# One visit for all eight chunks: regrouping the small products of a chunked recurrence beside a stream of projections

## The chip, the cores and the metric

One NeuronCore of one Trainium2 chip. The metric is the device time of one launch in microseconds. A core has five engines with queues of their own: TensorE (PE; its weight loads are shown as PEld), VectorE (DVE), ScalarE (ACT), GpSimd (POOL) and SyncE (SP). Each works through its queue in order; they meet at semaphores.

## The reference

A two-layer encoder over 512 tokens of width 1024. In each layer five branches read the same input h, each is gated and projected, and their sum goes through an output projection and a layer norm. Four branches are attention of some kind. The branch that matters here is a recurrence with a state S of 64 x 64 per head, for eight heads, run forward in time (e = 0) and backward (e = 1):

```
sa_t = S a_t
S    = S * w_t + sa_t b_t^T + v_t k_t^T
y_t  = S r_t
```

Here a = -kk (the normalised key), w is the decay, b = kk times a gate, and k is the key scaled by that gate. The two directions' outputs are added, normalised per head, and gated. The merge is

```
terms.append(sigmoid(h @ w_gate_i + b_gate_i) * (branch_i @ w_branch_i))
```

## The kernel before

All matmuls of the projections split each float32 operand into two parts and add three products of 512 columns (`gemm3_steps`, lines 149 to 151); the weights are loaded by SP (line 125) and split by ACT (line 135) and DVE (line 136). The tile framework allocates buffers by tag and orders each engine's queue ahead of time by a schedule of its own that follows the program's order where several instructions are ready.

**The recurrence** (`recurrence()`, from line 716) takes the 512 tokens in eight chunks of 64, two heads (128 partitions) at a time. A unit is one pair of heads `p` in one direction `e`; there are eight units in a layer. Within a chunk the recurrence becomes small matrix products and the inverse of a triangular 64 x 64 matrix; between chunks a state is carried.

- `pair_start(p)` projects k, r and v of the pair (`mixed`, lines 734 to 740).
- `early(p, e)` (line 802) makes the decays: running sums (line 820), the sums before and after each step (lines 824 to 833, tiles `bef`, `aft`), their exponentials, and the operands A0 and BK. Then, for two halves `c2` of four chunks each, the score products (line 881) go into two PSUM banks, `ps_s()` (tag psc, two banks) and `ps_m()` (tag pm, one bank). ACT copies 32-row blocks of them into NS (lines 890, 893), DVE masks the rest into MB and OM (lines 894, 896), and MB times the values goes into another `ps_m()` (line 902, helper line 92) and from there into Z (line 903). After both halves it makes B2 and K2, the operands at a chunk's end: `comp` through Exp (line 908), and products with it (lines 910, 912). They are transposed (line 921) and copied into OM (line 927).
- `late(p, e)` (line 945) inverts the 32-wide diagonal blocks of all chunks at once in a loop of 31 steps on DVE (lines 956 to 965, first transpose line 953), extends them to 64 (lines 978 to 990), and then, again for two halves of four chunks: px = WD x Z (line 1009) copied into WA and UV (lines 1012, 1015), WA x OM (line 1024) plus A0 into PE_ (line 1027), OM x UV (line 1035), and then the chain of states, chunk after chunk: a product of PE_ with the last state ST (line 1042), and its copy into the other ST by ACT and DVE (lines 1044, 1045). The results go to SY. px, both products of line 1024 and that of line 1035 use `ps_t()` (tag pt, two banks).
- `finish(p)` (line 1058) adds the outputs and gates them. It uses the bank pm too.

**The order of the work** is written by hand with generators. Every `yield` in these functions is a place where one step of other work is put in: the driver calls `pull(1)` (line 1114), which takes one step, three matmuls, from `fill()` (line 396), the gate and output projections of the other four branches (`branch_steps`, line 370; its PSUM bank is tag pf, its gating lines 380 to 390). A layer has 368 such steps: 8 output blocks times (8 + 4) for three branches and (8 + 2) for one. The attention part pulls 27 of them earlier by fractions (lines 623 and 702). What is left when the recurrence has ended runs at once (lines 1115, 1116), and then follow the projections of the recurrence's own branch and the output projection. In the recurrence `late(units[n])`, `finish` of the pair before, and `early(units[n + 1])` take turns, a yield each:

```
1106  while live:
1107      for g in list(live):
1108          if next(g, 0) == 0:
1109              live.remove(g)
1110          else:
1111              yield
```

Yields of a layer: 3 for each pair_start, 14 for each early, 24 for each late, 5 for each finish (4 for the last): 12 + 112 + 192 + 19 = 335.

Tiles of 128 x 512 in early() come from one rotating set, `tmp` (line 713), of 6 buffers.

## Time and profile before

| | |
|---|---|
| median of 3 runs | 2260.67 us (2260.49 to 2261.9) |
| the profiled execution | 2261.37 us |
| its span, first to last instruction | 2259.6 us |
| granted TensorE clock | 0.999 of full speed |
| recurrence of layer 0, and of layer 1 | 524 to 1032 us, 1623 to 2131 us |
| one pair of units, as an example | 714 to 842 us |

Busy time is the share of a stretch in which an engine executed an instruction; for PE the ends of matmuls are modelled, so the starts of successive ones tell more. In a row of a group, "x16 | 11.0, 685 | 0.0" is the count, the busy time in us, the mean of one in ns, and the idle time before them.

### The profile page before, as it was taken

To read this page: it belongs to the slowest core of one execution; us is meant where nothing else is said; L and a number is where in the kernel's file an instruction comes from. 1 tells how busy PE (TensorE), PEld (TensorE's weight loads), DVE (VectorE), ACT (ScalarE), POOL (GpSimd) and SP (SyncE) were. 2 spreads that over 40 slices of the span, in tenths; PEclk is the share of its full clock that TensorE was granted. 3 is DMA by queue.
4 is the path that set the end of the run, shared out by engine and by line. 5 is a ranking of instruction groups with operands and counts; after the bars stand their busy time and mean duration, and the time that the engine had idled before them with its cause. 6 is when DMAs were issued, how large, how long until landed. Compare 5 with 4: busy or idle time off the path is not lost.

```text
span 2259.6 us, 36239 instructions
## 1 busy us (share of the span) xinstructions
PE 2186.5 (97%) x13056; PEld 1678.6 (74%) x13056; DVE 1730.6 (77%) x4236; ACT 1273.2 (56%) x2785; POOL 59.6 (3%) x117
## 2 busy tenths in 40 slices
PE   6999999999999999999999999999999999999998
PEld 5777777777767777777787777777777777777776
DVE  7677887677989797975568778766788979879565
ACT  3565666676665555644326656677675646565440
POOL 0000000100000000000000000001000000000000
PEclk9999999999999999999999999999999999999999
DMA  7732124322222221315333312333313213222261
GB/s 261 222 108 91 56 80 112 113 86 85 75 80 66 86 88 59 102 49 181 117 115 108 98 62 70 97 106 89 112 57 99 71 62 98 72 80 73 84 195 38
DMA packets 111780, 220.49 MB, mean 98 GB/s; under 512 B 13240, under 2 KB 23224, under 8 KB 111216
## 3 DMA queue, kind: packets, MB, share of 16 engines
q1 hardware_dynamic: 101456, 195.09, 27.0%
q0 software_dynamic: 10144, 23.08, 4.0%
q8 instruction: 103, 1.69, 0.3%
q14 instruction: 77, 0.63, 0.1%
HBM read 187.66 MB, written 27.31 MB: 95 GB/s over the span
## 4 chain that ended last, share of the span: by engine, by line
PE 70%; DVE 14%; ACT 8%; DMA 5%; issue 3%; DVEq 0%; POOL 0%; ACTq 0%; SPq 0%
PE pg L150 10%; PE pg L151 10%; PE pg L149 10%; PE pf L149 6%; PE pf L150 5%; PE pf L151 5%; PE psc L444 4%; PE po L489 3%; PE pt L470 3%; DVE W L965 2%; DVE pr L963 2%; DMA wrawr<-in_w_out_dram 1%; DVE wlof L136 1%; PE po L479 1%; DMA wrawf<-in_w_mem_dram 1%
## 5 line engine op out<-in xcount | busy, mean ns | idle before, releaser
L149 PE MATMUL pg<-hT,whir 128*128 128x512 f32 (+1 forms) x912 | 364.0, 399 | 3.2 <-DVE kl L436 1.4
L150 PE MATMUL pg<-hT,whir 128*128 128x512 f32 (+1 forms) x912 | 365.4, 401 | 0.5 <-DVE hT L176 0.5
L151 PE MATMUL pg<-hT,wlor 128*128 128x512 f32 (+1 forms) x912 | 363.8, 399 | 2.1 <-DVE wlor L136 2.1
L136 DVE TENSOR_TENSOR wlor<-wrawr,whir 128x512 fp32r<-128x512 f32 x240 | 163.9, 688 | 114.8 <-ACT whir L135 104.9
L135 ACT CAST whir<-wrawr 128x512 fp32r<-128x512 f32 x240 | 147.7, 618 | 175.1 <-PE pg L150 116.7
L135 ACT CAST whif<-wrawf 128x512 fp32r<-128x512 f32 (+1 forms) x272 | 164.4, 605 | 135.4 <-PE pf L150 77.9
L149 PE MATMUL pf<-hT,whif 128*128 128x512 f32 x512 | 220.8, 431 | 3.4 <-DVE gt L388 2.8
L136 DVE TENSOR_TENSOR wlof<-wrawf,whif 128x512 fp32r<-128x512 f32 (+1 forms) x272 | 181.4, 669 | 49.2 <-ACT whif L135 43.2
L150 PE MATMUL pf<-hT,whif 128*128 128x512 f32 x512 | 206.7, 404 | 0.0
L151 PE MATMUL pf<-hT,wlof 128*128 128x512 f32 x512 | 205.2, 401 | 0.0
L149 PEld LDWEIGHTS pg<-hT,whir 128*128 128x128 f32 x912 | 172.0, 189 | 40.6 <-issue 3.0
L151 PEld LDWEIGHTS pg<-hT,wlor 128*128 128x128 f32 x912 | 171.9, 188 | 40.0 <-DVE wlor L136 4.9
L150 PEld LDWEIGHTS pg<-hT,whir 128*128 128x128 f32 x912 | 171.9, 189 | 37.8 <-issue 3.9
L176 DVE TENSOR_TENSOR pT<-pt,pT 128x512 fp32r<-128x512 f32 x176 | 114.2, 686 | 34.2 <-ACT pT L175 33.1
L175 ACT CAST pT<-pt 128x512 fp32r<-128x512 f32 x176 | 94.7, 589 | 63.0 <-PE pt L470 61.7
L149 PEld LDWEIGHTS pf<-hT,whif 128*128 128x128 f32 x512 | 96.5, 188 | 35.8 <-DVE gt L388 10.2
L470 PE MATMUL pt<-cst,p 128*128 128x128 f32 x704 | 118.6, 273 | 0.5 <-DVE p L461 0.5
L151 PEld LDWEIGHTS pf<-hT,wlof 128*128 128x128 f32 x512 | 96.4, 188 | 22.2 <-issue 1.6
L963 DVE TENSOR_TENSOR pr<-W,U 128x60 f32<-128x60 f32 (+24 forms) x496 | 103.5, 209 | 11.4
L965 DVE TENSOR_TENSOR W<-W,pr 128x60 f32<-128x60 f32 (+24 forms) x496 | 102.9, 208 | 11.0
L470 PEld LDWEIGHTS pt<-cst,p 128*128 128x128 f32 x704 | 89.8, 141 | 28.4 <-DVE p L461 3.6
L150 PEld LDWEIGHTS pf<-hT,whif 128*128 128x128 f32 x512 | 96.8, 189 | 18.8 <-issue 4.3
(326 smaller groups left out, 4809.1 us busy)
## 6 DMA issues: line engine op xcount, KB each, us to landing
wrawr<-in_w_in_dram SPq DMA_DIRECT2D x224, 256.0 KB, 2.8
wrawf<-in_w_gate_dram SPq DMA_DIRECT2D x160, 256.0 KB, 2.8
o<-scr_o POOLq DMA_DIRECT2D x26, 512.0 KB, 4.5
wrawf<-in_w_branch_dram SPq DMA_DIRECT2D x48, 256.0 KB, 2.7
bias<-scr_toe SPq DMA_DIRECT2D x24, 448.0 KB, 3.3
scr_o<-os SPq DMA_DIRECT2D x20, 512.0 KB, 3.7
wrawf<-in_w_in_dram SPq DMA_DIRECT2D x32, 256.0 KB, 3.0
wrawr<-in_w_out_dram SPq DMA_DIRECT2D x32, 256.0 KB, 2.9
```

The lines of the kernel that those rows point to most:

```text
L135: nc.scalar.copy(hi, raw)
L136: tt(lo, raw, f(hi), ALU.subtract)
L149: mm(ps, ah, bh, start=(i == 0), stop=False)
L150: mm(ps, ah, bl, start=False, stop=False)
L151: mm(ps, al, bh, start=False, stop=(i == n - 1))
L175: nc.scalar.copy(hi, src)
L176: tt(lo, src, f(hi), ALU.subtract)
L444: mm(ps[:, :nk], q[:, i, sl], part[:, i if g is None else g, :nk], start=(j == 0), stop=(j == 1))
L470: nc.tensor.transpose(pt[:, qb * 128:(qb + 1) * 128], p4[qb][:, kb * 128:(kb + 1) * 128], ident)
L489: mm(po, vwin(kb), pT[:, b, :], start=(kb == 0 and b == 0), stop=(kb == nkb - 1 and b == 1))
L963: tt(pr, W[:, t8, s:s + 1].to_broadcast([128, nt, n]), U[:, s:s + 1, rsl].to_broadcast([128, nt, n]), ALU.mult)
L965: tt(W[:, t8, rsl], W[:, t8, rsl], pr, ALU.add)
```

## The change

Four things. (1) In early() the score products of all eight chunks are made in one go, into four PSUM banks (psc, pm, psc, pg) where it was two banks for four chunks, and MB times the values goes into one bank and leaves it in one copy. MB is taken from the tmp set, whose buffers go from 6 to 5. (2) Of `bef` and `aft` only the one that is needed as the exclusive sum is made, and `comp` goes away: B2 and K2 are made from BK, which already holds the inputs times exp(+incl), times the chunk's total decay `gc`. (3) In late() each product is made for all eight chunks before the next: px (two banks), WA x OM (into both psc banks, which early() uses too, instead of pt), one add for each of two banks of 512 columns, OM x UV (both pt banks), then the chain of eight states without a break. WA, UV and PE_ double in size. (4) The yields between the halves go: late() yields 22 times instead of 24; early() still 14 times.

```diff
             def tmp(n="tmp"):
-                return rp.tile([128, S], F32, name=n, tag="tmp", bufs=6)
+                return rp.tile([128, S], F32, name=n, tag="tmp", bufs=5)
...
-                    bef = tmp()
-                    tt(bef, csum, s2, ALU.subtract)
-                    aft = tmp()
-                    tt(aft.rearrange("p (c t) -> p c t", t=64), tot.to_broadcast([128, 8, 64]),
-                       csum.rearrange("p (c t) -> p c t", t=64), ALU.subtract)
+                    excl = tmp()
                     if e == 0:
-                        incl, excl, comp = csum, bef, aft
+                        tt(excl, csum, s2, ALU.subtract)
+                        incl = csum
                     else:
-                        tt(s2, aft, s2, ALU.add)
-                        incl, excl, comp = s2, aft, bef
+                        tt(excl.rearrange("p (c t) -> p c t", t=64), tot.to_broadcast([128, 8, 64]),
+                           csum.rearrange("p (c t) -> p c t", t=64), ALU.subtract)
+                        tt(s2, excl, s2, ALU.add)
+                        incl = s2
...
+                    pss = [(ps_s(), ps_m()), (ps_s(), ps_g())]
+                    for c in range(8):
+                        for h, ps in enumerate(pss[c // 4]):
+                            sl = slice(64 * h, 64 * h + 64)
+                            kb_ = BK[sl, c // 2, c % 2].rearrange("p s t -> p (s t)")
+                            mm(ps[:, c % 4 * 128:(c % 4 + 1) * 128], kb_, A0[sl, c, 1 - h::1 + h, :], start=True, stop=True)
+                    MBs = []
                     for c2 in range(2):
-                        pss = [ps_s(), ps_m()]
-                        MB = T("MB", [128, 2, 2, 128], 1)
-                        for j in range(4):
...
+                        MB = tmp().rearrange("p (h c x) -> p h c x", h=2, c=2)
+                        MBs.append(MB)
+                        for h, ps in enumerate(pss[c2]):
...
-                        pmv = ps_m()
+                    pmv = ps_m()
+                    for c2, MB in enumerate(MBs):
                         for h in range(2):
                             for c in range(2):
-                                j = 2 * h + c
+                                j = 4 * c2 + 2 * h + c
                                 mm_cols(pmv[:, j * 64:(j + 1) * 64], MB[:, h, c, :], vsw[:, 2 * c2 + c, 64 * h:64 * h + 64])
-                        nc.scalar.copy(Z[:, :, 2 * c2:2 * c2 + 2, 64:128],
-                                       pmv[:, 0:256].rearrange("p (h c j) -> p h c j", h=2, j=64))
+                    nc.scalar.copy(Z[:, :, :, 64:128].rearrange("p h (d c) j -> p d h c j", d=2),
+                                   pmv.rearrange("p (d h c j) -> p d h c j", d=2, h=2, j=64))
...
-                    act(comp, comp, AF.Exp, scale=-hc)
                     B2, K2 = ai, gx
-                    tt(B2, ai, comp, ALU.mult)
+                    gcu = gc.rearrange("p (c u o) -> p c u o", u=2, o=1)
+                    tt(cu(B2), bv[:, :, 0::3, :], gcu.to_broadcast([128, 4, 2, 64]), ALU.mult)
                     for u in range(2):
-                        tt(cu(K2)[:, :, u, :], cu(ke)[:, :, 1 - u, :], cu(comp)[:, :, 1 - u, :], ALU.mult)
+                        tt(cu(K2)[:, :, u, :], bv[:, :, 2 - u, :], gcu[:, :, 1 - u, :].to_broadcast([128, 4, 64]), ALU.mult)
...
-                    n = 0
-                    for c2 in (0, 1) if e == 0 else (1, 0):
-
-                        WA = T("WA", [128, 2, 2, 64], 1)
-                        UV = T("UV", [128, 2, 2, 2, 64], 1)
...
+                    WA = T("WA", [128, 2, 2, 2, 64], 1)
+                    UV = T("UV", [128, 2, 2, 2, 2, 64], 1)
...
+                    for d in range(2):
                         px = ps_t()
...
-                        nc.scalar.copy(WA, px4[:, :, :, 0:64])
+                        nc.scalar.copy(WA[:, d], px4[:, :, :, 0:64])
                         for u in range(2):
                             rw = slice(64 * u, 64 * u + 64)
-                            nc.scalar.copy(UV[rw, :, :, u, :], px4[rw, :, :, 64:128])
-                        yield
...
-                        pss = [ps_t(), ps_t()]
...
+                            nc.scalar.copy(UV[rw, d, :, :, u, :], px4[rw, :, :, 64:128])
+                    yield
+
+                    PE_ = T("PE", [128, 8, 128], 1)
+                    pss = [ps_s(), ps_s()]
+                    for c in range(4):
                         for u, ps in enumerate(pss):
...
-                        ps = ps_t()
+                            rw = slice(64 * u, 64 * u + 64)
+                            for h in range(2):
+                                mm(ps[64 * h:64 * h + 64, c * 128:(c + 1) * 128], WA[rw, c // 2, h, c % 2, :],
+                                   OM[rw, h, 2 * c + u, :], start=True, stop=True)
+                    for u, ps in enumerate(pss):
+                        tt(PE_[:, u::2].rearrange("p c (x t) -> p c x t", x=2),
+                           ps.rearrange("p (c x t) -> p c x t", c=4, x=2), A0[:, u::2, 0:2], ALU.add)
+
+                    pcs = [ps_t(), ps_t()]
+                    for d in (0, 1) if e == 0 else (1, 0):
                         for j in range(4):
...
-                        yield
+                    yield
+                    n = 0
+                    for d in (0, 1) if e == 0 else (1, 0):
+                        ps = pcs[d]
                         for j in range(4) if e == 0 else range(3, -1, -1):
                             blk = ps[:, j * 128:(j + 1) * 128]
                             if n:
-                                mm(blk, PE_[:, j, :], ST[(n - 1) % 2], start=False, stop=True, skip_group_check=True)
+                                mm(blk, PE_[:, 4 * d + j, :], ST[(n - 1) % 2], start=False, stop=True, skip_group_check=True)
```

## Rows read from the trace of the kernel before

**Rows 1.** The page, part 1: busy time, share of the span, instructions.
```profile
PE 2186.5 (97%) x13056; PEld 1678.6 (74%) x13056; DVE 1730.6 (77%) x4236; ACT 1273.2 (56%) x2785; POOL 59.6 (3%) x117
```

**Rows 2.** Busy time by stretch: stretch, length, then each engine's busy us (instructions), clock, DMA.
```profile
core 0: us, PE busy (x) PEld busy (x) DVE busy (x) ACT busy (x) POOL busy (x), PEclk, DMA share, GB/s
524.00:1032.00 508.00, 493.29 (x3685) 368.89 (x3684) 419.25 (x1132) 290.06 (x695) 6.81 (x14) 1.00 0.24 76
714.00:743.00 29.00, 27.87 (x226) 21.15 (x219) 25.28 (x91) 14.43 (x38) 0.00 (x0) 1.00 0.15 48
...
787.00:809.00 22.00, 20.86 (x155) 15.70 (x154) 20.06 (x69) 10.50 (x28) 1.61 (x3) 1.00 0.48 156
809.00:842.00 33.00, 32.28 (x237) 23.61 (x237) 30.84 (x72) 21.75 (x49) 0.00 (x0) 1.00 0.24 77
714.00:842.00 128.00, 123.84 (x927) 93.45 (x921) 106.99 (x284) 72.84 (x173) 2.15 (x4) 1.00 0.26 82
1032.00:1135.00 103.00, 101.51 (x429) 79.97 (x429) 59.17 (x99) 40.59 (x67) 1.07 (x2) 1.00 0.47 154
```

**Rows 3.** The chain that ended last, in 714 to 743 and in 809 to 842.
```profile
by line: DVE pr L963 18.9%; DVE W L965 18.6%; issue 10.6%; DVE wlof L136 8.9%; DVE WD L970 6.0%; DVE ST L1045 5.8%; DVE wlor L136 4.7%; PE pt L1009 3.1%; DVE U L977 3.1%; DVE PE L1027 2.6%; DVE y L390 2.4%; DVE kes L941 2.4%; PE pf L151 2.3
...
by line: PE pf L149 23.5%; PE pf L150 19.6%; PE pf L151 18.3%; PE pm L881 6.6%; PE psc L881 4.0%; PE pm L92 3.5%; PE po L1066 3.3%; PE pm L1071 2.6%; PE pm L199 2.6%; PE psc L921 2.4%; PE pt L981 2.4%; ACT gt L380 2.1%; ACT whif L135 1.9%; 
```

**Rows 4.** Timeline of PE: start us, length us, what, count.
```profile
1009.11 0.40 PE L150 MATMUL pf<-hT,whif 128*128 128x512 f32 x1
1009.44 1.13 PE L1024 MATMUL pt<-OM,WA 64*64 64x128 f32 x16
...
1012.01 0.50 PE L149 MATMUL pf<-o,whif 128*128 128x512 f32 x1
1012.35 0.39 PE L150 MATMUL pf<-o,whif 128*128 128x512 f32 x1
1012.57 0.40 PE L151 MATMUL pf<-o,wlof 128*128 128x512 f32 x1
```

**Rows 5.** Waits of PE's weight loads, 560 to 1032: us in total, times, longest.
```profile
PEld pt L1042 <- DVE ST L1045: 11.9, 29, 0.8
PEld pt L1035 <- DVE PE L1027: 8.1, 12, 1.4
...
PEld pt L1024 <- ACT WA L1012: 3.3, 9, 0.4
```

**Rows 6.** Stretch behind the recurrence, instructions on the fill's bank pf alone.
```profile
1032.00:1060.00 28.00, 5.13 (x19) 3.58 (x19) 0.69 (x1) 0.68 (x1) 1.00 0.69 222
```

**Rows 7.** Timeline of DVE; in brackets idle time before, and what ended it.
```profile
717.85 0.76 DVE L1027 TENSOR_TENSOR PE<-pt,AR 128x256 f32<-128x256 f32 x2 [0.73 <-PE pt L1024]
...
772.91 1.28 DVE L136 TENSOR_TENSOR wlof<-wrawf,whif 128x512 fp32r<-128x512 f32 x2
```

**Rows 8.** Groups of instructions by line: count, busy us, mean ns, idle before.
```profile
L136 DVE TENSOR_TENSOR wlof<-wrawf,whif 128x512 fp32r<-128x512 f32 (+1 forms) x272 | 181.4, 669 | 49.2 <-ACT whif L135 43.2 <-PE pf L151 4.3 <-PE psc L444 0.4
...
L390 DVE TENSOR_TENSOR y<-y,gt 128x512 f32<-128x512 f32 x48 | 33.0, 687 | 0.5
L388 DVE SCALAR_TENSOR_TENSOR gt<-gt,pf 128x512 f32<-128x512 f32 x48 | 32.8, 684 | 7.6 <-PE pf L151 7.1
...
L1012 ACT COPY WA<-pt 128x256 f32<-128x256 f32 x32 | 11.9, 371 | 17.2 <-PE pt L1009 16.6
...
L827 DVE TENSOR_TENSOR tmp<-tmp 128x512 f32<-128x512 f32 x16 | 11.0, 685 | 0.0
...
L908 ACT ACTIVATE tmp<-tmp 128x512 f32<-128x512 f32 x16 | 10.0, 627 | 3.2 <-DVE tmp L825 3.1
```

**Rows 9.** Timelines of ACT and of DVE, 777 to 788.
```profile
777.58 0.25 ACT L890 COPY NS<-psc 32x128 f32<-32x128 f32 x1 [3.25 <-PE pm L881]
...
785.04 0.20 ACT L893 COPY NS<-pm 32x64 f32<-32x64 f32 x1
...
787.02 1.24 DVE L953 STREAM_TRANSPOSE U<-NS 128x1024 f32<-128x1024 f32 x1
```

More of the change, by code (lines that the diff above doesn't have):

```diff
@@ L995, in late @@
                     SY = q["sy"]
-                    n = 0
-                    for c2 in (0, 1) if e == 0 else (1, 0):
-                        WA = T("WA", [128, 2, 2, 64], 1)
-                        UV = T("UV", [128, 2, 2, 2, 64], 1)
-                        for u in range(2):
-                            rw = slice(64 * (1 - u), 64 * (1 - u) + 64)
-                            nc.scalar.copy(UV[rw, :, :, u, :],
-                                           vsw[rw, 2 * c2:2 * c2 + 2].rearrange("p c (h j) -> p h c j", h=2))
+                    WA = T("WA", [128, 2, 2, 2, 64], 1)
+                    UV = T("UV", [128, 2, 2, 2, 2, 64], 1)
+                    for u in range(2):
+                        rw = slice(64 * (1 - u), 64 * (1 - u) + 64)
+                        for h in range(2):
+                            nc.scalar.copy(UV[rw, :, h, :, u, :],
+                                           vsw[rw].rearrange("p (d c) x -> p d c x", d=2)[:, :, :, 64 * h:64 * h + 64])
+                    for d in range(2):
                         px = ps_t()
@@ L1013, in late @@
                         for u in range(2):
                             rw = slice(64 * u, 64 * u + 64)
-                            nc.scalar.copy(UV[rw, :, :, u, :], px4[rw, :, :, 64:128])
-                        yield
-                        PE_ = T("PE", [128, 4, 128], 1)
-                        pss = [ps_t(), ps_t()]
-                        for c in range(2):
-                            for u, ps in enumerate(pss):
-                                rw = slice(64 * u, 64 * u + 64)
-                                for h in range(2):
-                                    mm(ps[64 * h:64 * h + 64, c * 128:(c + 1) * 128], WA[rw, h, c, :],
-                                       OM[rw, h, 4 * c2 + 2 * c + u, :], start=True, stop=True)
@@ L1026, in late @@
-                        for u, ps in enumerate(pss):
-                            tt(PE_[:, u::2].rearrange("p c (x t) -> p c x t", x=2),
-                               ps[:, 0:256].rearrange("p (c x t) -> p c x t", c=2, x=2),
-                               A0[:, 4 * c2 + u:4 * c2 + 4:2, 0:2], ALU.add)
-                        ps = ps_t()
+                            nc.scalar.copy(UV[rw, d, :, :, u, :], px4[rw, :, :, 64:128])
+                    yield
+                    PE_ = T("PE", [128, 8, 128], 1)
@@ new lines, in late @@
+                    pss = [ps_s(), ps_s()]
+                    for c in range(4):
+                        for u, ps in enumerate(pss):
+                            rw = slice(64 * u, 64 * u + 64)
+                            for h in range(2):
+                                mm(ps[64 * h:64 * h + 64, c * 128:(c + 1) * 128], WA[rw, c // 2, h, c % 2, :],
[3 more added lines that the diff above has]
+                           ps.rearrange("p (c x t) -> p c x t", c=4, x=2), A0[:, u::2, 0:2], ALU.add)
@@ L1034, in late @@
                                 for o in (0, 64):
-                                    mm(ps[o:o + 64, j * 128 + h * 64:j * 128 + h * 64 + 64], OM[:, h, 4 * c2 + j, o:o + 64],
-                                       UV[:, h, j // 2, j % 2, :], start=(j == h == 0), stop=True,
+                                    mm(pcs[d][o:o + 64, j * 128 + h * 64:j * 128 + h * 64 + 64], OM[:, h, 4 * d + j, o:o + 64],
+                                       UV[:, d, h, j // 2, j % 2, :], start=(j == h == 0), stop=True,
                                        skip_group_check=True)
-                        yield
+                    yield
+                    n = 0
+                    for d in (0, 1) if e == 0 else (1, 0):
+                        ps = pcs[d]
                         for j in range(4) if e == 0 else range(3, -1, -1):
```

10 lines of the change are left out of this document (2 added, 8 removed).

## The prediction

> **What bounds the kernel now.** The page comes first: TensorE (PE) is busy for 97% of the span, DVE for 77% [rows 1]. A busy PE counts modelled ends, so this does not yet say that PE is the limit. Then the stretches [rows 2]: the recurrence and the fill that is laid between its steps take 508 us of the first layer, and the second repeats it, so 1016 us of the 2260; all that the diff touches lies there. A pair of units (both directions of one head pair) lasts 128 us, 714 to 842 for instance; a layer has four pairs, the kernel eight. In a pair the reader is to see two regimes. From 714 to 743 and from 787 to 809 DVE is busy for 25.28 of 29 and 20.06 of 22 us: that is the loop of 31 steps for the 32-wide inverses (lines 956 to 965). Between them lie the projections of the next heads and early(), and from 809 to 842 PE and DVE are both full. The chain says the same by name [rows 3]: in the first stretch it runs over DVE's pr and W, in the last over PE's fill and small groups, which add up to 88% in its row.
>
> Then PE's queue, group by group [rows 4]. Fill matmuls of 512 columns start every 0.23 us. A small group between them costs more than itself: about 0.10 us is lost ahead of it (1009.11 to 1009.44 is 0.33), and the first fill matmul after it takes 0.34 again (1012.01 to 1012.35); with some 0.1 lost behind the group's own last start, which is my estimate, a visit costs 0.3 us. That is what "one visit" can remove. Last, what PE's weight loads wait for in the recurrence of a layer [rows 5]: the state chain's copies (11.9 us), and L1035 on the adds of L1027 (8.1), because L1035's bank is one that those adds have to empty first.
>
> **The change, part by part.** Costs are per unit (one head pair in one direction); there are sixteen.
>
> *Yields.* late() yields 24 times before (8 in the loop, 2, and 14 in its halves) and 22 times after (8, 2, and 2 + 10). Each yield pulls one fill step, three matmuls, 0.69 us at 0.23. So 32 steps, 22.1 us of PE, leave the recurrence and run behind it. That the fill follows the yields shows in its count: 335 yields and 27 steps of earlier pulls make 362 of a layer's 368 steps, so 6 steps, 18 matmuls, should be left at the end; 19 are seen after 1032 [rows 6]. Behind the recurrence nothing covers them: PE is busy for 101.5 of 103 us there [rows 2]. I book +22.1; bounds 0 (the order fills ahead) and 22.1. The recurrence has to shrink by 22.1 / 8 = 2.8 us a pair before anything is won.
>
> *714 to 743, DVE.* Four adds of 256 columns, of which two take 0.76 us, so 1.52, become two of 512, about 1.28 as two splits of that width take [rows 7]: 0.24 saved. The two fill steps take their vector work along: 3 splits of 0.669, a multiply of 0.684 and an add of 0.687 [rows 8] per 12 steps, 3.38 / 12 = 0.28 a step, 0.56. Together 0.8. Bounds: 0.2 (the adds alone) and 2.0 (also the 0.73 that DVE waits for L1024 here [rows 7], and more than half a visit).
> Merging the adds has a price too: the first half's adds are done after 0.76 us now, and all after 1.28 then, so the first state product that needs them could start 0.5 us later. DVE is full in this stretch, so I don't book it. The Trainium skill (Perfetto Trace Analysis, Optimizing Scalar/DVE Operations) says that where the vector engines are not saturated but make bubbles on other engines, breaking instructions up may let work finish sooner. By that rule 16 x 0.5 = 8 us would come back, and the sum below would end at 2245 instead of 2237; the row of a full DVE speaks against its condition here.
>
> *787 to 809, DVE.* The same terms: 0.8, bounds 0.2 and 2.0.
>
> *760 to 787, the way to the next inverse.* Today the second half's score matmuls (L881) need the bank pm, which the first half's scores and then its MB product hold. So the NS copies run in two bursts, from 777.58 and to 785.24, and the inverse's first transpose (L953) starts at 787.02 [rows 9]. With four banks all scores come at once; 16 copies, half of 0.25 and half of 0.20, need 3.7 us back to back and could end near 781.5, 3.7 us sooner. PE's fill of this stretch has still to be done, so I take just over half: 2.0, bounds 0 and 3.7. One subtract of 512 columns falls away (L827, 0.685 [rows 8], 0.6 from start to start) in an unbroken run of DVE that leads to the scores: 0.6, bounds 0 and 0.6. Sum 2.6. B2 and K2 keep their sizes and only read other tiles.
>
> *809 to 842, PE.* Scores, MB products, px, WA x OM and OM x UV each go from two visits to one, five visits of 0.3 a unit; three of them (0.9) and one of the two fill steps (0.7) fall here: 1.6. Bounds 0.6 (two visits) and 3.2 (all that two units' visits could give).
>
> *743 to 760, projections.* 0, bounds 0 and 0.7 (one fill step).
>
> *Costed at nothing.* The Exp of L908 (0.627 [rows 8]) and the halving of the Z copies: ACT is busy for 73 of 128 us [rows 2], and PE's fill hides them; uncovered they would add a gain of 0.6 or more a unit. The number of PE's small matmuls: unchanged. The waits of L1035 on L1027: both its banks are now freed by the px copies ahead of L1024, so this wait should go, but what is late next is the same DVE queue, at the first state product; 16.2 us for both layers is the bound, and the upper bounds above hold it. In return the adds' two banks are psc, which early() uses: a matmul of early() that waits for one holds up the fill steps behind it in PE's queue, and the copies and adds that follow it on ACT and DVE. No row shows that wait; the nearest is L1035 on L1027, 0.7 on average (8.1 / 12). tmp shrinks from 6 buffers to 5 and now also holds MB: the next pair's small weights are loaded into a tmp tile, which three projections cover. No DMA is added or moved on SP's or POOL's queue.
>
> **Sum.** A pair: 0.8 + 2.6 + 0.8 + 1.6 = 5.8; eight pairs 46.4 saved; 22.1 given back; net 24.3. The profiled execution's own time is 2261.37 us (its span 2259.6 and 1.8 around it), 0.7 above the median of the runs shown: 2237. With every lower bound 1.0 a pair, 8 - 22.1: 2275. With every upper bound 12.2 a pair, 98 - 22: 2185.
>
> **Rivals.**
> (a) *DVE keeps the length: slower.* The inverse loop and what stands around it in DVE's queue set the pace in 714 to 743, in 787 to 809 and also in 809 to 842, where DVE is busy for 30.84 of 33 [rows 2]. PE's savings become idle time, and the fill steps come back in full behind. Then at most 0.8 + 0.8 a pair counts, 12.8 us, at the lower bounds 3.2: 9 to 19 more than now, 2270 to 2280. It decides if a pair shrinks by less than 2.8 us. For it: DVE is busy for 107 of 128 us. Against it: the chain in 809 to 842 is PE's.
> (b) *The evacuation in bulk.* Six copies out of px (2 WA, 4 UV, 0.37 each [rows 8]) stand together ahead of L1024, 1.1 us more than now, and the psc banks stay taken through the adds, up to 0.7: 1.1 to 1.8 a unit, 18 to 29 us of the gain, 2255 to 2266. For it: L1024 waits for WA already [rows 5]. Against it: a fill step stands in between. The Trainium skill (Perfetto Trace Analysis, Matmuls) says the like: independent groups should rotate through different banks, so that evacuating one overlaps the next one's matmuls. No row here shows the merged form.
> (c) *The change does less than it says.* finish() holds pm while early() of the second direction runs, and MB's second tile may find no free tmp buffer; then scores and MB products stay two visits. The 2.0 and half of the 1.6 go, 22 us: 2259.
> (d) *More:* all visits and the waits of L1035 count, under 2208.
>
> **How the numbers follow.** The forecast, ending between 2208 and 2256: 0.62. (d): 0.08. (b) and (c): 0.13 together, most of it no change. (a): 0.17. A measurement of this kernel tells about 0.2%, 4.5 us, from no change. So faster 0.70, same 0.12, slower 0.18. The range 2208 to 2270 leaves out (d) and most of (a), 0.2 in all at most.
>
> **What would show it.** Right: 16 more fill steps, 48 matmuls, behind the recurrence in each layer; a pair of 122 us; L953 some 5 to 6 us after the first NS copy, not 9.4, in the stretch like 777 to 787; no wait of L1035 on the adds. Wrong: a pair of 126 us or more with DVE as full as now (a); psc matmuls that wait for the adds, or L1024 that waits over 1 us for ACT (b); L881 in pieces as now (c). The granted clock has to stay at full speed; if it falls, the sum does not hold.

## The result, and the profile after

The changed kernel is slower: 2310.65 us (median of 4 runs, 2301.85 to 2320.92) against 2260.94 for the kernel before on the same chip. The ratio is 1.0225, with a 95% interval of 1.0203 to 1.0247. The forecast was 2237, and the range to 2270 does not hold it. Its four runs lie 19 us apart, with granted clocks from 0.974 to 0.983; those of the kernel before lie 1.4 us apart. The profiled execution took 2316.03 us, with a span of 2314.3 and a mean granted clock of 0.976 (0.999 before).

Page of the changed kernel, part 1, which answers to [rows 1]:

```profile
PE 2184.1 (94%) x13056; PEld 1694.1 (73%) x13056; DVE 1728.2 (75%) x4188; ACT 1259.2 (54%) x2753; POOL 59.4 (3%) x117
```

PE's busy time is what it was (2186.5). So the 54.7 us by which the span grew show as idle time of PE: 2314.3 - 2184.1 = 130.2, where it was 73.1. But the change was to shorten PE's busy time, and that it stayed the same hides a part of the loss, as the last experiments show. DVE and ACT are no busier. Which stretches pay shows in the windows of the changed kernel (columns as in [rows 2]; 717 to 846 is the pair that ran from 714 to 842 before, 1600 to 2190 holds the recurrence of layer 1):

```profile
717.00:846.00 129.00, 122.78 (x929) 95.21 (x928) 105.21 (x278) 71.24 (x170) 2.15 (x4) 0.96 0.26 81
978.00:1066.00 88.00, 80.85 (x619) 60.54 (x613) 52.33 (x140) 38.82 (x90) 0.25 (x1) 0.94 0.28 90
1600.00:2190.00 590.00, 546.03 (x3950) 417.55 (x3949) 460.92 (x1210) 327.76 (x776) 7.25 (x14) 0.96 0.25 78
```

The column to look at is the clock. It was 1.00 in every stretch of [rows 2] and is 0.94 to 0.96 now, in both layers. The pair lasts 129 us where 122 was forecast. The fill steps behind the recurrence are as forecast in number, and dearer. These are the instructions on the bank pf, in the stretch from the last state product to the last of these steps, first in the kernel before, then in the changed one (compare [rows 6]):

```profile
1024.60:1041.00 16.40, 10.16 (x36) 6.62 (x36) 0.84 (x2) 1.36 (x2) 1.00 0.20 60
```

```profile
1031.00:1066.00 35.00, 25.93 (x84) 17.74 (x84) 1.37 (x2) 2.05 (x3) 0.85 0.45 149
```

84 matmuls instead of 36 are the 48 foreseen. The stretch, in which finish() and the first projections behind it run too, takes 35.0 us instead of 16.4, at a clock of 0.85.

**Where the clock first falls.** Both kernels come to the same place soon after the first unit has begun, and only the changed one loses its clock there. PE's timeline of the kernel before (columns as in [rows 4])

```profile
555.42 0.39 PE L151 MATMUL pf<-hT,wlof 128*128 128x512 f32 x1
555.65 0.39 PE L150 MATMUL pg<-hT,whir 128*128 128x512 f32 x1
555.88 0.39 PE L151 MATMUL pg<-hT,wlor 128*128 128x512 f32 x1
...
558.67 0.40 PE L151 MATMUL pg<-hT,wlor 128*128 128x512 f32 x1
558.96 0.50 PE L149 MATMUL pf<-o,whif 128*128 128x512 f32 x1
559.30 0.39 PE L150 MATMUL pf<-o,whif 128*128 128x512 f32 x1
```

and of the changed kernel, with idle time and what ended it in brackets:

```profile
555.80 0.40 PE L151 MATMUL pf<-hT,wlof 128*128 128x512 f32 x1
558.82 0.50 PE L149 MATMUL pf<-o,whif 128*128 128x512 f32 x1 [2.62 <-ACT gt L380]
559.16 0.39 PE L150 MATMUL pf<-o,whif 128*128 128x512 f32 x1
559.38 0.59 PE L151 MATMUL pf<-o,wlof 128*128 128x512 f32 x1
559.77 0.63 PE L149 MATMUL pf<-o,whif 128*128 128x512 f32 x1
560.20 0.63 PE L150 MATMUL pf<-o,whif 128*128 128x512 f32 x1
```

In both, the fill has ended a block and its only bank, pf, waits until ACT has read it (L380). In the kernel before PE fills these 3.3 us with fourteen products into the bank pg: they are projections of the next pair, which run ahead. In the changed kernel there is nothing between, PE stands idle for 2.62 us, and from 559.77 on 512 columns start every 0.43 us instead of 0.23: that is the lower of the two clock levels, 1.2 GHz. By windows of the changed kernel:

```profile
556.00:559.00 3.00, 0.38 (x2) 0.18 (x2) 2.99 (x7) 2.76 (x5) 0.00 (x0) 1.00 0.19 59
559.00:563.00 4.00, 4.00 (x11) 2.71 (x12) 3.92 (x8) 0.62 (x1) 0.00 (x0) 0.57 0.00 0
```

The wait for ACT is not new. In the changed kernel's ACT queue three exponentials of early() stand ahead of the read of pf:

```profile
556.52 0.63 ACT L849 ACTIVATE tmp<-tmp 128x512 f32<-128x512 f32 x1
557.06 0.61 ACT L854 ACTIVATE tmp<-tmp 128x512 f32<-128x512 f32 x1
557.58 0.61 ACT L859 ACTIVATE tmp<-tmp 128x512 f32<-128x512 f32 x1
558.10 0.67 ACT L380 ACTIVATE gt<-pf,hb 128x512 f32<-128x512 f32 x1
```

Before there were four (L908 among them). What is gone is the work that hid it. Instructions on the bank pg from 550 to 560, kernel before, then changed:

```profile
550.00:560.00 10.00, 3.42 (x14) 2.63 (x14) 0.00 (x0) 0.00 (x0) 1.00 0.17 53
```

```profile
550.00:560.00 10.00, 0.00 (x0) 0.00 (x0) 0.00 (x0) 0.00 (x0) 0.97 0.17 53
```

What PE itself waited for in layer 0, from 524 to 1066 (us in total, times, longest), kernel before, then changed, shows that such waits grew:

```profile
PE pf L149 <- ACT gt L380: 2.5, 6, 0.7
```

```profile
PE pf L149 <- ACT gt L380: 10.1, 6, 3.6
PE pt L1046 <- DVE ST L1049: 6.0, 11, 1.2
PE pf L149 <- DVE gt L388: 4.5, 8, 0.9
```

In the kernel before, no single idle time of PE in this stretch is longer than 1.03 us. In the changed kernel four are of 1.94 to 3.58 us, at 558.82, 646.58, 900.52 and 1042.07. Not all of them end with the read of pf: that at 900.52 ends with a weight split (L135). The granted clock is low behind some pairs of shorter ones too, 0.83 from 580 to 590 us behind idle times of 1.50 and 1.36 us.

So the theory that the experiments had to test: the fourth bank of the scores is one of the two banks of pg. The scheduler gives out the buffers of a tag in the order of the program, and the next pair's projections stand behind this early()'s scores in it; so they can no longer run ahead, PE has nothing to do while pf waits, and its clock falls.

### The profile page after: what moved, and what is told of

It is laid out like the page before. It is cut to its first block, busy times and chain, and to the rows that moved or that the text cites. A ratio compares the mean times of both kernels' runs of the same rounds, so it can differ in the third digit from the quotient of the medians.

```text
span 2314.3 us, 36122 instructions
## 1 busy us (share of the span) xinstructions
PE 2184.1 (94%) x13056; PEld 1694.1 (73%) x13056; DVE 1728.2 (75%) x4188; ACT 1259.2 (54%) x2753; POOL 59.4 (3%) x117
## 4 chain that ended last, share of the span: by engine, by line
PE 49%; issue 37%; DVE 6%; ACT 4%; DMA 3%; DVEq 0%; SPq 0%; ACTq 0%; POOLq 0%; POOL 0%
PE pg L151 9%; PE pg L150 9%; PE pg L149 9%; PE psc L444 4%; PE po L489 3%; PE pt L470 3%; DMA o<-scr_o 2%; PE pf L149 1%; PE psc L149 1%; PE pf L150 1%; PE psc L151 1%; PE psc L150 1%; PE po L479 1%; PE pf L151 1%; DMA wrawf<-in_w_mem_dram 1%
## 5 line engine op out<-in xcount | busy, mean ns | idle before, releaser
L135 ACT CAST whif<-wrawf 128x512 fp32r<-128x512 f32 (+1 forms) x272 | 164.5, 606 | 192.3 <-PE pf L150 102.5
L149 PE MATMUL pf<-hT,whif 128*128 128x512 f32 x512 | 226.0, 441 | 23.1 <-DVE gt L388 9.0
L135 ACT CAST whir<-wrawr 128x512 fp32r<-128x512 f32 x240 | 147.8, 619 | 175.0 <-PE pg L150 130.3
L150 PE MATMUL pf<-hT,whif 128*128 128x512 f32 x512 | 208.6, 407 | 0.0
L149 PEld LDWEIGHTS pf<-hT,whif 128*128 128x128 f32 x512 | 99.6, 195 | 59.7 <-DVE gt L388 20.7
L149 PE MATMUL pf<-o,whif 128*128 128x512 f32 x224 | 104.1, 465 | 20.3 <-ACT gt L380 20.3
L150 PEld LDWEIGHTS pf<-hT,whif 128*128 128x128 f32 x512 | 99.7, 195 | 20.1 <-issue 3.8
```

The lines of the kernel that those rows point to most:

```text
L135: nc.scalar.copy(hi, raw)
L149: mm(ps, ah, bh, start=(i == 0), stop=False)
L150: mm(ps, ah, bl, start=False, stop=False)
```

## The experiments

Each text that was written ahead of a run names the theories as they stood then. Times are medians; the ratio is to the kernel before as measured beside each run (medians of 2258.33 to 2260.94 us), with its 95% interval; clock is that of the profiled execution.

| run | us | ratio | clock |
|---|---|---|---|
| early() of the change, late() of before | 2309.44 | 1.0213 (1.0191 to 1.0235) | 0.983 |
| changed, late() yields 24 times | 2300.62 | 1.0178 (1.0162 to 1.0195) | 0.986 |
| changed, pf and pg one set of three | 2305.77 | 1.0194 (1.0174 to 1.0213) | 0.980 |
| before, six fill steps ahead | 2249.48 | 0.9950 (0.9933 to 0.9967) | 0.998 |
| changed, six fill steps ahead | 2284.63 | 1.0114 (1.0099 to 1.0129) | 0.985 |
| before with the ends alone | 2246.81 | 0.9943 (0.9928 to 0.9958) | 0.998 |
| before with the scores' visit alone | 2311.51 | 1.0228 (1.0212 to 1.0243) | 0.983 |
| before, one bank's tag changed | 2315.91 | 1.0251 (1.0236 to 1.0267) | 0.982 |
| scores' visit alone, pt for pg | 2258.95 | 0.9999 (0.9990 to 1.0008) | 0.993 |
| changed, pt for pg | 2269.88 | 1.0046 (1.0032 to 1.0060) | 0.991 |
| changed, scores in halves | 2273.63 | 1.0069 (1.0052 to 1.0086) | 0.992 |
| changed, scores in halves, 24 yields | 2257.05 | 0.9993 (0.9983 to 1.0002) | 0.996 |
| changed, pt for pg, 24 yields | 2250.94 | 0.9962 (0.9948 to 0.9976) | 0.996 |
| scores in halves, 24 yields, six ahead | 2245.29 | 0.9938 (0.9924 to 0.9953) | 0.998 |
| ends alone, six ahead | 2247.29 | 0.9938 (0.9925 to 0.9952) | 0.998 |
| ends alone, twelve ahead | 2261.89 | 1.0009 (1.0000 to 1.0018) | 0.995 |
| changed, pt for pg, 24 yields, six ahead | 2239.75 | 0.9912 (0.9898 to 0.9925) | 0.997 |

One more kernel, the changed late() beside the early() of before with its six tmp buffers, has no time: its buffers need 114.6 KB a partition where 113.6 are left. So late() was never measured without the ends.

**First: which part carries it, and is it the forecast's rival (a).** When these ran, the bank pg was not yet suspected; it was known that PE idles and the clock falls.

The changed kernel with late() as before (its halves, its pt banks, its 24 yields):

```diff
-                    for d in range(2):
-                        px = ps_t()
...
+                    for c2 in (0, 1) if e == 0 else (1, 0):
+                        WA = T("WA", [128, 2, 2, 64], 1)
...
```

> The new early() (four score banks, MB from tmp, B2 and K2 from BK, tmp of 5) with the old late(). Theory 1 (the loss is the granted clock: with the new order of the queues PE stands idle for 1.3 to 3.6 us where the fill's only bank pf waits for its gating, and runs at 1.2 GHz for a while after): the part that makes those waits carries the loss, so one of the two parts alone costs 25 to 50 us with a mean clock of 0.98 to 0.99, and a part that leaves the clock at 1.00 costs nothing (within 5 us of 2261) or gains. Theory 2 (the bulk evacuation of merged groups is slow by itself): each part costs its own share, about 10 to 40 us, at whatever clock.

2309.44 us: early() with the ends loses 48.9 us by itself, nearly all of the change's 49.7. The changed kernel with its two yields put back into the loops:

```diff
                             nc.scalar.copy(UV[rw, d, :, :, u, :], px4[rw, :, :, 64:128])
-                    yield
+                        yield
...
                                        skip_group_check=True)
-                    yield
+                        yield
                     n = 0
```

> The changed kernel with late() yielding 24 times again (a yield after each half of px and of OM x UV). The fill behind the recurrence goes back to about 18 matmuls. If the returned fill steps are the loss (rival (a) of the prediction): 22 us back, about 2289. Theory 1: the fill's block ends meet other places of the queues; the time follows the clock, 2240 to 2310, about 0.5 us lost for each us at half clock. Theory 2: within 8 us of 2311 less the tail's 22.

2300.62, 10.0 us better; the two intervals just miss each other. So the 32 fill steps that went behind the recurrence are about a fifth of the loss, and rival (a), which had them come back in full, does not explain it. The third gave the fill more banks, as one set with pg:

```diff
-        return pp.tile([128, 512], F32, name="pg", tag="pg", bufs=2)
+        return pp.tile([128, 512], F32, name="pg", tag="pg", bufs=3)
...
-        return pp.tile([128, 512], F32, name="pf", tag="pf", bufs=1)
+        return pp.tile([128, 512], F32, name="pf", tag="pg", bufs=3)
```

> The changed kernel with pf and pg as one set of three banks, so that a fill block need not wait until the last one is gated. Theory 1: the waits of pf on L380, L386 and L388 (some 35 us in a layer by PE and its weight loads) shrink by more than half, the clock returns to 0.99 or 1.00, and the time falls by 25 us or more, to 2240 to 2285. Theory 2: the waits go, the time falls by under 15 us, the clock's effect is small.

2305.77: a miss for the first theory. PE's wait for L380 in layer 0 does shrink, from 10.1 to 3.4 us, but a new one has come, a score product (L877) that waits once for 7.4 us (for DVE's L863), and the clock stays at 0.980. That one common set ties still more work to one order would explain it, but no run shows it.

**Second: placement, the ends, the scores.** A shift of the fill by six steps moves every block boundary of the fill against the recurrence, and so tests whether the place of the waits is luck:

```diff
+            pull(6)
             for _ in recurrence():
                 pull(1)
```

In the kernel before:

> The kernel before, with nothing changed but that six steps of the fill are pulled ahead of the recurrence, so that every fill block ends at another place of early() and late(). Theory 1a (the kernel before lies in a good alignment between the ends of the fill's blocks and the busy places of ACT's and DVE's queues; any change of order loses it): the clock falls here too, to 0.98 or 0.99, and the time rises by 20 to 50 us. Theory 1b (it is the new grouping that makes PE stand idle, wherever the fill's blocks end): the clock stays at 1.00 and the time within 8 us of 2261.

In the changed kernel:

> The changed kernel with six steps of the fill pulled ahead of the recurrence. Theory 1a: the gaps move with the ends of the fill's blocks, other places, another time, anything from 2240 to 2320, and the clock goes with it. Theory 1b: within 10 us of 2311.

Before: 2249.48, a gain of 10 (2259.56 beside it), a little past the second range, its clock whole at 0.998; so the kernel before does not owe its clock to this one placement. Changed: 2284.63, 26 us better than unshifted and still a clock of 0.985; placement decides about part of the loss, not about its being there. Then the change in two pieces, each alone in the kernel before. The ends:

```diff
-                    act(comp, comp, AF.Exp, scale=-hc)
                     B2, K2 = ai, gx
-                    tt(B2, ai, comp, ALU.mult)
+                    gcu = gc.rearrange("p (c u o) -> p c u o", u=2, o=1)
+                    tt(cu(B2), bv[:, :, 0::3, :], gcu.to_broadcast([128, 4, 2, 64]), ALU.mult)
...
```

> The kernel before with only the operands at a chunk's end changed: B2 and K2 from BK and gc, one of the two decay differences and the Exp of comp gone. Scores and late() as before. Theory 1a: any new order may lose the clock, so 2280 to 2310 with the clock below 0.99. Theory 1b: less work and the same grouping, so 2240 to 2261 with the clock at 1.00.

2246.81: a gain of 13 us at a clock of 0.998. The scores' visit, with MB in tmp (6 buffers) and one copy to Z:

```diff
-                    for c2 in range(2):
-                        pss = [ps_s(), ps_m()]
+                    pss = [(ps_s(), ps_m()), (ps_s(), ps_g())]
+                    for c in range(8):
...
```

> The kernel before with only the scores' visit changed (four banks, MB from the tmp set of 6, one copy into Z). Theory 1a: 2280 to 2310 with the clock below 0.99, no worse than the ends alone. Theory 1b: the loss sits here, 2290 to 2310, with gaps of PE between the scores and the products that wait for their evacuation.

2311.51: this piece alone loses as much as the whole change (52 us). It has two properties that differ from before: all eight chunks at once, and a bank of pg.

**Third: the bank or the size.** This pair tells them apart. In the kernel before, with every product still in halves, only a tag:

```diff
-                        pmv = ps_m()
+                        pmv = ps_g()
```

> The kernel before with nothing regrouped: the two products of MB with the values go into a bank of the set pg in place of the bank pm. No instruction is added or taken away. Theory P (pg): the loss of the change comes from the two banks of pg, which the next pair's projections need to run ahead while the fill's bank waits; whatever early() puts into pg ties them to the place of early() in the program. Then this kernel loses most of what the changed kernel loses, although all its products are still in halves: 2280 to 2310 us, a granted clock of 0.975 to 0.99, and no product into pg between 555 and 559 us. Rival S (size): the loss comes from making all eight chunks' scores at once, sixteen copies in one stretch of ScalarE. Then the bank does not matter: 2255 to 2265 us, clock 0.998 to 1.0.

In the scores' visit alone, the other way round:

```diff
-                    pss = [(ps_s(), ps_m()), (ps_s(), ps_g())]
+                    pss = [(ps_s(), ps_m()), (ps_s(), ps_t())]
```

> The kernel before with the scores of all eight chunks in one visit (the part that by itself lost 51 us), with one difference to that kernel: the fourth bank is taken from the set pt, not from pg. Theory P (pg): the products into pg run ahead again between 555 and 559 us, the clock stays at 0.997 or more, and the time is 2245 to 2265 us. Rival S (size): 2295 to 2315 us with a clock of 0.975 to 0.99 as with pg.

The tag alone, with no instruction added or removed, costs more than the whole change, and more than was expected: 2315.91, ratio 1.0251. Its PE timeline, at the place shown above:

```profile
553.73 0.40 PE L151 MATMUL pf<-hT,wlof 128*128 128x512 f32 x1
557.27 0.79 PE L149 MATMUL pf<-o,whif 128*128 128x512 f32 x1 [3.14 <-ACT gt L380]
557.86 0.63 PE L150 MATMUL pf<-o,whif 128*128 128x512 f32 x1
```

and its windows around it:

```profile
551.00:554.00 3.00, 3.00 (x14) 2.21 (x12) 3.00 (x5) 1.74 (x6) 0.00 (x0) 1.00 0.26 83
554.00:557.00 3.00, 0.13 (x1) 0.00 (x0) 3.00 (x7) 3.00 (x6) 0.00 (x0) 0.93 0.16 58
557.00:563.00 6.00, 5.73 (x15) 4.21 (x16) 4.47 (x8) 1.45 (x3) 0.00 (x0) 0.50 0.00 0
```

A full clock, then 3 us in which ACT and DVE are busy throughout and PE hardly, then 0.50. No product is on pg from 550 to 560 us here either. Its page, part 1:

```profile
PE 2204.4 (95%) x13056; PEld 1694.0 (73%) x13056; DVE 1739.2 (75%) x4236; ACT 1276.4 (55%) x2785; POOL 59.3 (3%) x117
```

These are the same instructions as in the kernel before, so this page shows the price of the waits without any saving beside it: of the 56.5 us by which the span grew (2316.1 against 2259.6), PE is busy for 17.9 more and idle for 38.6 more.

With all eight chunks at once but pt for pg the time is 2258.95, no change (the clock, 0.993, a little under what was expected), and the fourteen products on pg are back (that kernel, bank pg, 550 to 560):

```profile
550.00:560.00 10.00, 3.42 (x14) 2.64 (x14) 0.00 (x0) 0.00 (x0) 1.00 0.13 43
```

So it is the bank, not the size. That the products on pg go with the tag and come back without it is shown; that the order in which buffers are given out is the reason was not looked at by itself. The Trainium skill (Perfetto Trace Analysis, Matmul Optimizations) advises using all eight PSUM banks for the most parallelism. Both kernels do (pg, psc and pt two each, pf and pm one each); which stage gets which bank decides here, by 57.6 us in the tag run, and of that the rule says nothing.

The same one-line repair in the whole change:

> The changed kernel with the scores' fourth bank from the set pt in place of pg; everything else of the change stays. Theory P (pg): clock 0.997 or more and 2230 to 2255 us, since the ends' part alone gave 13 us and the rest of what was foreseen is then left; faster than the kernel before. Rival S (size): no more than 10 us better than the changed kernel, 2295 to 2315 us.

2269.88 is 40.8 us better than the change and between the two ranges: the bank is worth most of the loss, but the repaired change was to beat the kernel before, and does not. The changed late() and ends with the scores in halves, as in the kernel before:

> The changed kernel with the scores in two halves as before (banks psc and pm, MB with a buffer of its own); the ends from BK and late() in one visit stay. Theory P (pg) and rival S (size) agree here that the loss goes: 2225 to 2250 us with a clock of 0.997 or more. The ends alone gave 2247 us; below that is what late() in one visit is worth, above it what it costs. If the clock falls again with pg free, late() has a loss of its own and both theories are short.

2273.63, where both theories had 2250 at most. As the last sentence of that text has it, late() has a loss of its own and both theories are short.

**Fourth: late()'s loss.** In that kernel the steps behind the recurrence meet this (PE's timeline):

```profile
1014.64 0.80 PE L151 MATMUL pf<-hT,wlof 128*128 128x512 f32 x1
1015.27 0.40 PE L151 MATMUL pg<-hT,wlor 128*128 128x512 f32 x1
1019.00 0.80 PE L149 MATMUL pf<-o,whif 128*128 128x512 f32 x1 [3.33 <-ACT gt L380]
1019.60 0.63 PE L150 MATMUL pf<-o,whif 128*128 128x512 f32 x1
```

and ACT at that time:

```profile
1014.97 1.28 ACT L204 ACT_TABLE_LOAD   x1
1016.26 0.69 ACT L204 ACTIVATE ysq<-pm,eps 128x512 f32<-128x512 f32 x1
1016.97 1.28 ACT L380 ACT_TABLE_LOAD   x1
1018.26 0.69 ACT L380 ACTIVATE gt<-pf,hb 128x512 f32<-128x512 f32 x1
```

finish() of the last pair takes a root (L204), which needs another function table than the gating; the read of pf stands behind two table loads, PE idles for 3.33 us and goes on at the lower clock (0.63 for a product, where 0.40 is usual). The next run puts the two yields back there (the edit of the second run above):

> The changed late() and ends with the scores in halves as before (2273.6 us), and late() yielding 24 times again as before: the two yields that the change folded together stand in their loops again. Theory R (returned fill): of what is left of the loss, most is the price of the 16 fill steps per layer that went behind the recurrence, where the one bank pf waits for its gating and the clock falls (28 steps took 34.9 us there, 12 took 16.0). Then the tail is 12 steps again and the time is 2235 to 2252 us with a clock of 0.997 or more. Rival L (late itself): the loss sits in late() (its banks psc, the longer stretch of copies), and the yields give no more than their 0.69 us each, 22 us at most but with the clock still under 0.995: 2255 to 2270 us.

2257.05, 16.6 us better. The clock of 0.996 lies between the two theories (0.997 or more, under 0.995), the time is in the range of rival L: most of late()'s loss were the returned steps (PE's longest wait for L380 in layer 0 is 0.7 us here, where it was 3.3), and some 10 us against the ends alone are left. The whole change with both repairs:

> The whole change with the two repairs: the scores' fourth bank from pt in place of pg, and 24 yields in late(). Theory R: 2238 to 2256 us, faster than the kernel before, at a clock of 0.995 or more. Rival L: 2258 to 2270 us.

2250.94, in the range of theory R and a little faster than the kernel before: ratio 0.9962, interval 0.9948 to 0.9976. And six fill steps ahead, in the run with the scores in halves:

> The kernel of the first of these runs with six more fill steps run just ahead of the recurrence (in the kernel before that alone gave 11 us). Theory R: half of the 12 steps left behind it go to a place where they cost 0.69 us and not 1.2 to 1.3: 3 to 11 us below the first of these runs, 2230 to 2245 us. Rival L: no more than 4 us below it.

2245.29, 11.8 better, a little more than was expected.

**Fifth: what adds up.** The ends alone with six steps ahead:

> The kernel before with the two edits that gave something alone, and nothing else of the change: the ends from BK (2246.8 us alone) and six fill steps ahead of the recurrence (2249.5 us alone). If the two gains are of different places (vector work in the recurrence, and the steps behind it), they add: 2234 to 2239 us. If both are one and the same thing, the end of the recurrence coming before the fill has run out, it stays at 2243 to 2248 us.

2247.29, the second case of that text: the two gains of 13 and 10 us do not add at all. With twelve steps ahead:

> The same with twelve fill steps ahead, so that none is left when the recurrence has ended. If a step behind the recurrence costs 1.2 to 1.3 us and ahead of it 0.69: another 3 to 8 us less than with six. If PE needs some steps there beside finish of the last pair, whose products wait for ScalarE and VectorE, it stands idle there and this is the same or slower than with six.

2261.89, 14.6 us lost again: the time of that text's second case, but not by its reason. The trace has the loss inside the recurrence: from the second inverse of layer 0 to the third (first transposes at 609.21 and 665.93 us) it takes 56.7 us, where it took 47.0 with six. In between DVE reads pf late, PE stands idle and the clock falls (PE's timeline, then the window around it):

```profile
646.73 0.80 PE L149 MATMUL pf<-hT,whif 128*128 128x512 f32 x1 [3.65 <-DVE gt L388]
```

```profile
645.00:650.00 5.00, 3.27 (x8) 2.60 (x9) 4.91 (x9) 0.62 (x1) 0.00 (x0) 0.58 0.17 53
```

With six steps ahead no idle time of PE in layer 0 is that long (none of 1.9 us or more). Here pg is free and seven products on it fill the start of the wait; the single bank pf still costs time where a block of the fill ends at a bad place. So the place matters even with pg free.

The whole change, both repairs and six steps ahead:

> The whole change with both repairs (2250.9 us) and six fill steps ahead. If what is gained there is as large as beside the other kernels (11.8 us beside the repaired late(), 11 beside the kernel before): 2238 to 2242 us. If late() in one visit costs some 10 us by itself (2257.1 us against 2246.8 for the ends alone), it stays above the first of these runs by 4 us or more.

2239.75, ratio 0.9912 (0.9898 to 0.9925): this version beats both kernels and lies in the first range. It is 7.5 us faster than the ends alone with six steps ahead. The run with late() but without the scores' visit stands between them (2245.29, ratio 0.9938 like that of the ends alone), so with six steps ahead late() in one visit costs nothing, and most of the 7.5 came with the scores' visit. Its page, part 1:

```profile
PE 2153.1 (96%) x13056; PEld 1664.7 (74%) x13056; DVE 1721.5 (77%) x4188; ACT 1258.6 (56%) x2753; POOL 59.6 (3%) x117
```

With the same 13056 products PE is busy for 31.0 us less than in the change as given, and idle for 85.5 us of the 2238.6 instead of 130.2. That splits the change's loss against this version roughly into 45 us of PE standing idle and 31 of slower or more scattered products.

## Why the prediction was wrong

**The step that failed** stands under 760 to 787: "With four banks all scores come at once". It costed the banks by who in early() and late() holds them now, and booked nothing for taking one of pg. It never asked who else uses pg, though line 736 of the kernel shows it: `mixed`, the projections of the next pair, which in the kernel before run while early() of the pair's second direction is still at work. What the runs showed in its place: a bank's tag alone costs 57.6 us (2315.91 against 2258.33), with pt for pg the scores' visit costs nothing (0.9999), and in the whole change the tag is worth 40.8 us. The time that the step promised, 2.0 us a pair from an earlier inverse, did not come either: in the example pair the scores began later, not sooner (below).

**The clock.** The text said that the sum does not hold if the clock falls, and gave that no chance. It should have been a rival: the fill's single bank waits for ACT in the kernel before already, and at the place shown only the products on pg keep PE at work. The Trainium skill (TensorE: Matmul & The Clock Gate, A second HAM failure mode: psum-queue depth-cycling) says the like of another kernel: short idle times of PE between groups of matmuls, from cycling through PSUM, make its clock swing between the two levels. The windows agree: 1.00 before the gap, 0.57 and 0.50 behind it.

**Point by point.**
- *Yields.* 48 more fill matmuls behind the recurrence in layer 0: right. Their price was booked at 22.1 us for both layers; putting them back gave 10.0 in the change, 16.6 and 18.9 in the kernels with pg free (2273.63 to 2257.05, 2269.88 to 2250.94). So the term was of the right size with pg free, somewhat high, and more than twice too high in the change. "PE is busy for 101.5 of 103 us there" was no guard against their own waits: the stretch grew by 1.16 us a step ((35.0 - 16.4) / 16), not 0.69.
- *One visit.* Right in kind: with the repairs and no shift PE is busy for 2165.4 us instead of 2186.5 (page of that kernel, below), 21.1 us less, or 1.3 a unit, where five visits of 0.3 are 1.5. But the ends alone, which save no visit, have 8.4 of them (second page). Against the ends alone the visits are worth 12.7 us, 0.8 a unit; with six steps ahead in both it is 27.1 (2180.2 to 2153.1), 1.7 a unit. The 0.1 us behind a group, which the text called its estimate, is shown by no run alone.

```profile
PE 2165.4 (96%) x13056; PEld 1673.3 (74%) x13056; DVE 1725.6 (77%) x4188; ACT 1259.3 (56%) x2753; POOL 59.8 (3%) x117
```

```profile
PE 2178.1 (97%) x13056; PEld 1679.0 (75%) x13056; DVE 1720.4 (77%) x4220; ACT 1265.0 (56%) x2769; POOL 59.3 (3%) x117
```

- *The terms as a sum.* The same kernel is the sum without its yields' term, so it should have been 46.4 us faster and was 8.1 (2250.94 against 2259.07). Of PE's 21.1, idle time took back 11.4 (84.5 against 73.1). The waits of PE's weight loads show one part of it (that kernel, 560 to 1040; its L1046 is L1042 of the kernel before, for which [rows 5] has 11.9):

```profile
PEld pt L1046 <- DVE ST L1049: 19.4, 35, 1.7
PEld pf L149 <- DVE gt L388: 7.8, 14, 1.5
```

  The chain of eight states waits longer for its copies. It is not the price that the text named, a first state product that waits for the merged adds: no row shows such a wait. How much of the time it is, was not tried alone.
- *The way to the next inverse.* Right as a distance, without effect: in the changed kernel the first NS copy comes at 785.07 and the transpose 5.66 us later, 5 to 6 foreseen, 9.4 before [rows 9]; but the copy itself starts 7.5 us later than in the kernel before, 2.9 of them because the pair does (its first transpose is at 717.14, not 714.29), the rest because its score products start late, at 783.76 instead of 776.38. The ACT and the DVE row:

```profile
785.07 0.25 ACT L890 COPY NS<-psc 32x128 f32<-32x128 f32 x1
```

```profile
790.73 1.24 DVE L954 STREAM_TRANSPOSE U<-NS 128x1024 f32<-128x1024 f32 x1
```

- *L1035 on the adds.* The wait [rows 5] is gone, as foreseen (the line is L1036 now).
- *The ends.* Booked at 0.6 a pair, 4.8 us, and nothing for the Exp of L908. Alone they gave 13 us: too small by more than half. The subtract was booked for one unit of a pair, but falls away in all sixteen: DVE is busy for 10.2 us less (1720.4 against 1730.6). The Exp of L908 stood in ACT's queue ahead of the read of pf, as shown above, but PE waits for that read as long without it (2.6 us in layer 0, 2.5 before). What of the 13 us comes from which was not tried by itself.
- *Rivals.* (a) gave 2270 to 2280 by DVE and returned steps; the time went past it by another mechanism, and DVE is no busier. Its sign, a pair of 126 us or more with DVE as full as now, did nearly show (129 us, DVE busy for 105.21 of them): as worded it cannot tell (a) from a falling clock. (b) is not answered by the bank, for its copies and its psc banks are in late(). Its signs hardly show in the changed kernel: in layer 0 the products of WA (L1025 now) wait for ACT's copies for 0.6 us at most, and once for an add, 1.1 us. That late() costs some 10 us beside the ends without a shift, and nothing with six steps ahead, has no shown reason. (c) falls: the sixteen NS copies of all four banks stand in one run, from 785.07 to 788.74.

**What stays open.** The pieces do not add: the ends gain 13 us and six steps ahead 10, together 13; late() in one visit loses 10 beside the ends (2257.05 against 2246.81) and nothing with six steps ahead (2245.29 against 2247.29). Which wait falls where is likely to be new with each edit, since the scheduler orders the queues anew; that was not tried apart. A remainder of some 10 us a kernel is not explained by any one row here.

## What to carry to other kernels

Before a stage takes a buffer from a rotating set, look for work further on in the program that runs ahead through that set, and for the waits that this work hides; a tag alone moved this kernel by 2.5%. When the bound engine has both a single-banked stream and a second stream that jumps in, the second one is not slack. And take apart a change with several edits: here one bank and two folded yields hid what the other parts gain.

## What had not been expected of the hardware

- After 2.62 us without a matmul PE was at 0.43 us for 512 columns, not 0.23, from the fourth product on, and in the tag run after 3.14 us the granted clock was 0.50 over the next 6 us. In the kernel before the granted clock stayed at 1.00 all through the recurrence. A wait of some 3 us so costs more than its own length.
- An engine's busy time can hide a loss: PE's was the same in the fast and in the slow kernel (2186.5 and 2184.1), since the parts that save PE's time gave about what slower products cost (in the tag run, which saves nothing, it rose to 2204.4). The clock column and the idle time told it.
- ACT's change between the functions of L204 and L380 cost 1.28 us each way, and both stood ahead of the one read that PE waited for.
